# Computing three more MLP units with seven half-size products instead of eight

## The chip, the cores and the metric

The kernel runs on one core of one Trainium2 chip. The metric is the device time of one execution in microseconds (us); several executions are timed and their median is taken. The time before is 2046.41 us, the median of 3 runs (2046.17 to 2046.44).

## The reference

Two blocks follow each other on one sequence of T = 512 tokens of width D = 1024, everything in float32. The first has two layers of sparse attention, a short convolution, a gated merge and an MLP; the second has one layer of dilated attention, an mLSTM and a gated FFN. Cut to what the change touches:

```
# first_block, for each of two layers
x = x + merged @ w_mix_out[l]
u = rmsnorm(x, norm_mlp[l])
x = x + square(relu(u @ w_mlp_up[l])) @ w_mlp_down[l]        # hidden width 4096
# second_block, its FFN
h = modulate(rms_norm(x, g_ffn), sh_f, sc_f)
x = x + gt_f * ((silu(h @ w_gate) * (h @ w_up)) @ w_down)    # hidden width 2816
```

## The kernel before, in words

Activations are kept transposed: x is eight tiles x[0] to x[7] of 128 (of D) by 512 (tokens). A float32 product is made of three float32r matmuls: each operand is split into hi (rounded to float32r) and lo (the rest), and hi·hi, hi·lo and lo·hi are summed in PSUM. The moving operand is a pair (hi, lo) of activations; the weights are loaded as raw blocks of 128x1024 numbers (512 rows by 256 columns), and `split` (L208) makes their hi by a cast on ScalarE (L222, tile wh) and their lo by a subtraction on VectorE (L223, tile wl). Pool whp holds four such pairs, pool rawp eight raw blocks, pool mmp four PSUM banks.

`linear` (L242) is the plain product: for each output tile, k = 0 to 7 and three matmuls of 512 columns each (L290 to L292). `seven` (L311) computes the same for a 2x2 arrangement of half-size blocks (K halved, tokens halved, two blocks of 256 output columns) with seven block products of 24 matmuls of 256 columns each (L412 to L414). Its weight operands are the raw blocks a, b (first 256 columns, upper and lower half of K), c, d (second 256 columns) and sums of them, tile ws; its moving operands are the plain halves of the activation and two mixed ones, ta[k] and tb[k] for k = 0 to 3. `mix` (L480) makes these of x[k] and x[k+4]: four VectorE steps of 128x256 (L487 to L490), then two hi casts on ScalarE (L466) and two lo subtractions on VectorE (L467). ta[3] and tb[3] need x[7], the last tile of the layer before.

The norm of an MLP is applied late: the tiles of u are x times the gain alone (`prep` L469, hi L474 on ScalarE and lo L475 on VectorE), and 1/rms, a column per token, is applied when a hidden tile is read from PSUM. For it `square` (L498) sums the squares of the eight tiles (L505 on ScalarE, L506 on VectorE), `rstd1` (L508) adds them over partitions on TensorE (L1072), takes the root on ScalarE (L513) and refines it on VectorE (L526 to L528), and `rstd2` (L518) spreads it over partitions by a matmul (L1083) and copies it to SBUF (L522).

An MLP has eight units of 512 hidden columns. Units 1 to 7 are computed by `seven` (`up`, L977) and interleaved with the down products of the unit before (`mesh`). Unit 0 is a plain `linear` (u0, L1002): the mixes of k = 0 to 2 are made while the last tiles of w_mix_out come out (`evmix`, L924), the mix of k = 3 in the background of unit 0 (L1005). The FFN has 11 units of 256 gate and 256 up columns; unit 0 and unit 1 are plain (`gateup`, L1551, unit 0 in two halves of tokens since the norm arrives in halves), the others are by `seven`. In the FFN the mixes are made in the background of gateup(1). The norm in the FFN is `ffn_norm` (L1154): column sums L1072, L1157 to L1159 on VectorE, a spread L1083, then L1093, L1103 and L1106 per tile.

The program text gives an order of pieces: `Prog.run` walks the list, fetches weights some units ahead and splits them two units ahead. The order on each engine is then settled by a scheduler when the program is built; each engine works through its queue in that order, and waits on semaphores for the others.

Of the kernel before, what the change touches and what calls it, by code (L numbers as in the profile page):

```python
# [15 lines left out]
P = 128  # L16
# [4 lines left out]
KT = D // P  # L21
# [105 lines left out]
def blocks_kernel(ctx: ExitStack, tc: tile.TileContext, a: dict, out: bass.AP, stop=None):  # L127
# [21 lines left out]
    def slot(dt=F32, w=T):  # L149
        return gp.tile([P, w], dt, tag="g", name=nm("g"))  # L150
# [157 lines left out]

        return ap.unsqueeze(1).to_broadcast([P, 2, H])

    def seven(srcs, xs, ta, tb, evac):  # L311

# [41 lines left out]
            4: {"make": lambda: raw["d"]},  # L356
        }

        def half(d, k0, t):
            return lambda k: [o[:, th(t)] for o in d(k0 + k)]  # L360

        def keep(n, b):
            def f():
                tmp[n] = slot()
                act.copy(tmp[n], bank[b])
            return f
# [18 lines left out]
        def e4():  # L385
            evac(1, 0, bank.pop("Y"), False)

        prods = [
            (1, "X", half(xs, 0, 0), keep(1, "X")),
            (5, "Z", half(ta, 0, 0), keep(5, "Z")),  # L390
            (6, "Y", half(tb, 0, 0), e6),
# [4 lines left out]
        ]  # L396
        pieces = []
        for n, b, mv, after in prods:
            first = n in (1, 5, 6)
            u = us[n]  # L400
            piece = [("unit", u)]
            for m in range(2):

                def emit(u=u, b=b, mv=mv, m=m, first=first):
                    if first and m == 0:
                        bank[b] = mmbank()
                    ps = bank[b][:, th(m)]
                    for k in range(4):
                        hi, lo = mv(k)
                        wh = u["hi"][:, k, m * P : (m + 1) * P]  # L410
                        wl = u["lo"][:, k, m * P : (m + 1) * P]
                        pe.matmul(ps, wh, hi, start=first and m == 0 and k == 0, stop=False, skip_group_check=True)  # L412
                        pe.matmul(ps, wh, lo, start=False, stop=False, skip_group_check=True)  # L413
                        S["pe"] = pe.matmul(ps, wl, hi, start=False, stop=k == 3, skip_group_check=True)  # L414

                piece.append(("do", emit))
            piece.append(("do", after))
            pieces.append(piece)
# [269 lines left out]
    def layer1(l, nextprep):  # L688
# [235 lines left out]
        def evmix(g):  # L924
            def f(j, ps, cs):
                j = 4 * g + j
                dve.tensor_add(x[j], ps, x[j])
                prep("n", j, col(C_NMLP + 8 * l + j))
                if 4 <= j < KT - 1:
                    for step in mix("n", j - 4, y):  # L930
                        step()
            return f
# [12 lines left out]

        NU = MLP_TILES // 4
        W_up = a["w_mlp_up"][l]

        def ev0(j, ps, cs):
            r = slot()  # L950
            dve.scalar_tensor_tensor(r, ps, 0.0, S["n", "rs"], op0=ALU.max, op1=ALU.mult)
            act.activation(r, r, AF.Square)
            hid[j] = hilo(r)

        def evup(c):
            def f(n, t, src, own):
# [18 lines left out]
            return f  # L975

        def up(c):  # L977
            return seven([(W_up, 512 * c), (W_up, 512 * c + 256)], xs, lambda k: S["n", "ta", k], lambda k: S["n", "tb", k], evup(c))

        def down(c, gs=(0, 1), n=1, last=False):  # L980

# [17 lines left out]
                S.pop(("n", "ta", k))  # L999
                S.pop(("n", "tb", k))  # L1000

        u0 = linear(W_up, 0, [4, 4], 0, [P] * 4, xs, ev0)  # L1002
        add(u0[:1])
        do(lambda: rstd1("n"))
        I.append(("bg", mix("n", 3, y)))  # L1005
        add(u0[1:3])
        do(lambda: rstd2("n"))
        add(u0[3:])
        I.append(("drain", None))
        do(ada_start)  # L1010
        I.append(("rate", 0.25))
        I.append(("bg", [ada(n) for n in range(24 * l, 24 * l + 24)] + ([ada_end] if l else [])))
# [150 lines left out]
    def block2():  # L1163
# [440 lines left out]
        def unit(c):  # L1604

            gt = {}

            def evac(n, t, src, own):
                if n == 0:
                    gt[t] = slot()  # L1610
                    act.activation(gt[t], src, AF.Silu)
                    if ("late", t) in gt:
                        finish_(t, *gt.pop(("late", t)))
                elif t in gt:
                    finish_(t, src, own)
                else:
                    gt["late", t] = (src, own)

            def finish_(t, src, own):
                r = gt.pop(t)  # L1620
                dve.tensor_mul(r, src, r)
                for m in range(2):
                    k_ = 2 * c + m
                    if k_ not in ff:
                        ff[k_] = (slot(F32R), slot(F32R))
                    hi, lo = ff[k_]
                    act.copy(hi[:, th(t)], r[:, th(m)])
                    dve.tensor_sub(lo[:, th(t)], r[:, th(m)], hi[:, th(t)].bitcast(F32))

            return seven([(a["w_gate_2"], 256 * c), (a["w_up_2"], 256 * c)], xs, lambda k: S["h", "ta", k],  # L1630
                         lambda k: S["h", "tb", k], evac)

        NG = FF_TILES // 2
        ND = (FF_TILES + 3) // 4
# [25 lines left out]
        add(u0[:2])  # L1660
        do(lambda: S.pop("rest")())
        I.append(("ahead", (3, 6)))
        add(u0[2:])
        I.append(("rate", 2.0))
        I.append(("bg", [f for k in range(4) for f in mix("h", k, lambda j: S.pop(("h", "y", j)))]))
        add(gateup(1, 1))
        I.append(("drain", None))
        I.append(("ahead", (2, 5)))
        for c in range(2, NG - 1, 2):
            I.extend(mesh(unit(c) + unit(c + 1), down(c // 2 - 1)))  # L1670
        I.extend(mesh(unit(NG - 1), down(ND - 2)))
# [107 lines left out]
```

## Time and profile before

| | |
|---|---|
| median of 3 runs | 2046.41 us |
| the profiled execution | 2044.83 us |
| its span, first to last instruction | 2043.0 us |
| TensorE busy | 2026.1 us, 99% |
| VectorE busy | 1547.0 us, 76% |
| ScalarE busy | 986.6 us, 48% |
| mean granted TensorE clock | 0.997 |

Matmuls are pipelined: a row's duration is longer than the distance to the next row, so the pace of TensorE is read from one start to the next. The same holds, by about 0.09 us, for VectorE and ScalarE. The clock column is the share of 2.4 GHz that was granted; 0.50 is 1.2 GHz.

### The profile page before, as it was taken

To read this page: it belongs to the slowest core of one execution; us is meant where nothing else is said; L and a number is where in the kernel's file an instruction comes from. 1 tells how busy PE (TensorE), PEld (TensorE's weight loads), DVE (VectorE), ACT (ScalarE), POOL (GpSimd) and SP (SyncE) were. 2 spreads that over 40 slices of the span, in tenths; PEclk is the share of its full clock that TensorE was granted. 3 is DMA by queue.
4 is the path that set the end of the run, shared out by engine and by line. 5 is a ranking of instruction groups with operands and counts; after the bars stand their busy time and mean duration, and the time that the engine had idled before them with its cause. 6 is when DMAs were issued, how large, how long until landed. Compare 5 with 4: busy or idle time off the path is not lost.

```text
span 2043.0 us, 29780 instructions
## 1 busy us (share of the span) xinstructions
PE 2026.1 (99%) x11632; PEld 1754.7 (86%) x11632; DVE 1547.0 (76%) x2783; ACT 986.6 (48%) x1713; POOL 19.5 (1%) x33
## 2 busy tenths in 40 slices
PE   9999999999999999999999999999999998999999
PEld 7888888899999888888888999999877797999998
DVE  6998667888787659977678888877777386777775
ACT  5323774644444432338655444455377754444442
POOL 0000000000000000000000000000010000000000
PEclk9999999999999999999999999999999999999999
DMA  7233223344444332331224444443221131332321
GB/s 248 83 94 102 73 63 93 100 149 149 150 155 147 105 105 83 100 96 63 73 93 134 145 155 134 155 134 88 87 83 54 50 114 32 104 103 94 114 94 42
DMA packets 203116, 216.62 MB, mean 106 GB/s; under 512 B 10720, under 2 KB 182112, under 8 KB 202976
## 3 DMA queue, kind: packets, MB, share of 16 engines
q1 hardware_dynamic: 202976, 214.73, 33.8%
q8 instruction: 91, 1.49, 0.3%
q14 instruction: 49, 0.40, 0.1%
HBM read 212.60 MB, written 2.10 MB: 105 GB/s over the span
## 4 chain that ended last, share of the span: by engine, by line
PE 95%; DVE 2%; ACT 1%; DMA 0%; issue 0%; SPq 0%; POOL 0%; DVEq 0%; ACTq 0%; POOLq 0%
PE mm L290 14%; PE mm L291 13%; PE mm L292 13%; PE mm L414 7%; PE mm L413 7%; PE mm L412 7%; PE at L290 7%; PE at L291 7%; PE at L292 7%; PE at L555 2%; PE mm L441 1%; PE mm L442 1%; PE mm L443 1%; PE ot L589 1%; PE at L574 1%; PE mm L1583 1%
## 5 line engine op out<-in xcount | busy, mean ns | idle before, releaser
L222 ACT CAST wh<-raw 128x1024 fp32r<-128x1024 f32 (+3 forms) x278 | 283.6, 1023 | 535.0 <-PE mm L413 221.6
L290 PE MATMUL mm<-g,wh 128*128 128x512 f32 (+2 forms) x1360 | 512.6, 378 | 1.7 <-ACT g L1103 1.6
L292 PE MATMUL mm<-g,wl 128*128 128x512 f32 (+2 forms) x1360 | 512.9, 377 | 0.0
L291 PE MATMUL mm<-g,wh 128*128 128x512 f32 (+2 forms) x1360 | 510.4, 375 | 0.0
L223 DVE TENSOR_TENSOR wl<-raw,wh 128x1024 fp32r<-128x1024 f32 (+3 forms) x278 | 329.3, 1186 | 141.3 <-ACT wh L222 140.3
L414 PE MATMUL mm<-g,wl 128*128 128x256 f32 x1288 | 364.6, 283 | 0.0
L413 PE MATMUL mm<-g,wh 128*128 128x256 f32 x1288 | 364.5, 283 | 0.0
L412 PE MATMUL mm<-g,wh 128*128 128x256 f32 x1288 | 363.9, 283 | 0.0
L290 PEld LDWEIGHTS mm<-g,wh 128*128 128x128 f32 x1360 | 255.8, 188 | 49.6 <-issue 4.3
L292 PEld LDWEIGHTS mm<-g,wl 128*128 128x128 f32 x1360 | 256.2, 188 | 45.5 <-issue 1.0
L291 PEld LDWEIGHTS mm<-g,wh 128*128 128x128 f32 x1360 | 256.1, 188 | 44.2 <-DVE g L475 0.3
L412 PEld LDWEIGHTS mm<-g,wh 128*128 128x128 f32 x1288 | 246.8, 192 | 4.7
L413 PEld LDWEIGHTS mm<-g,wh 128*128 128x128 f32 x1288 | 246.8, 192 | 4.6
L414 PEld LDWEIGHTS mm<-g,wl 128*128 128x128 f32 x1288 | 246.8, 192 | 0.2
L290 PE MATMUL at<-g,g 128*128 128x512 f32 x592 | 231.9, 392 | 0.0
L291 PE MATMUL at<-g,g 128*128 128x512 f32 x592 | 231.8, 392 | 0.0
L292 PE MATMUL at<-g,g 128*128 128x512 f32 x592 | 230.6, 389 | 0.1
L222 ACT CAST wh<-ws 128x1024 fp32r<-128x1024 f32 x69 | 72.3, 1048 | 182.3 <-PE mm L413 170.1
L292 PEld LDWEIGHTS at<-g,g 128*128 128x128 f32 x592 | 111.2, 188 | 24.7 <-DVE g L223 0.8
L223 DVE TENSOR_TENSOR wl<-ws,wh 128x1024 fp32r<-128x1024 f32 x69 | 84.5, 1224 | 59.7 <-ACT wh L222 59.7
L290 PEld LDWEIGHTS at<-g,g 128*128 128x128 f32 x592 | 111.7, 189 | 19.9
L291 PEld LDWEIGHTS at<-g,g 128*128 128x128 f32 x592 | 111.7, 189 | 18.6
(272 smaller groups left out, 2685.4 us busy)
## 6 DMA issues: line engine op xcount, KB each, us to landing
raw<-w_in SPq DMA_DIRECT2D x111, 512.0 KB, 3.8
raw<-w_mlp_up SPq DMA_DIRECT2D x64, 512.0 KB, 3.8
raw<-w_mlp_down SPq DMA_DIRECT2D x64, 512.0 KB, 3.6
g<-w_ada SPq DMA_DIRECT2D x96, 256.0 KB, 4.2
raw<-w_gate SPq DMA_DIRECT2D x22, 512.0 KB, 3.7
raw<-w_up SPq DMA_DIRECT2D x22, 512.0 KB, 3.6
raw<-w_down SPq DMA_DIRECT2D x22, 512.0 KB, 3.4
raw<-w_mix_out SPq DMA_DIRECT2D x16, 512.0 KB, 3.7
```

Of the source, the lines that this page charges most:

```text
L222: act.copy(hi, raw)
L223: dve.tensor_sub(lo, raw, hi.bitcast(F32))
L290: pe.matmul(ps, wh, hi[:, cs], start=st, stop=False)
L291: pe.matmul(ps, wh, lo[:, cs], start=False, stop=False)
L292: S["pe"] = pe.matmul(ps, wl, hi[:, cs], start=False, stop=en)
L412: pe.matmul(ps, wh, hi, start=first and m == 0 and k == 0, stop=False, skip_group_check=True)
L413: pe.matmul(ps, wh, lo, start=False, stop=False, skip_group_check=True)
L414: S["pe"] = pe.matmul(ps, wl, hi, start=False, stop=k == 3, skip_group_check=True)
L441: pe.matmul(ps, xh, wh, start=kb + k == 0, stop=False)
L442: pe.matmul(ps, xl, wh, start=False, stop=False)
L443: pe.matmul(ps, xh, wl, start=False, stop=kb + k == KT - 1)
L555: pe.matmul(ps[:, :WM], qs[hh][:, i * P : (i + 1) * P], ks[hh][n][:, :WM], start=n == 0, stop=n == 1)
```

## The change

`seven` gets a flag `late`, with another order of products and other weight sums: products 1, 2 and 3 come first (they need plain activations only), 5, 6, 7 and 4 after them, and product 3 takes a bank of its own. b - the lower half of the first columns - is turned in place into the operand of product 3. Unit 0 of both MLPs becomes `up(0)` with this flag, and the second FFN unit `unit(1)`. The mix of k = 3 moves from the background of unit 0 to the reading of x[7], and the FFN's mixes from the background of gateup(1) to places beside the second half of gateup(0).

```
+        def p2late():
+            dve.tensor_add(raw["b"], raw["b"], raw["a"])
+            dve.tensor_add(raw["b"], raw["b"], ws["s"])
+        if late:
+            us = {
+                1: {"load": get("a", "c"), "make": lambda: raw["a"]},
+                2: {"load": get("d", "b"), "make": lambda: raw["b"], "post": lambda: (p1(), p2late())},
+                3: {"make": lambda: raw["b"]},
+                5: {"make": lambda: ws["s"], "post": p5},
+                6: {"make": lambda: ws["s"], "post": p6},
+                7: {"make": lambda: raw["c"]},
+                4: {"make": lambda: raw["d"]},
+            }
...
+            (1, "X", half(xs, 0, 0), keep(1, "X")),
+            (2, "X", half(xs, 4, 0), e2),
+            (3, "Z", half(xs, 4, 1), lambda: None),
+            (5, "V", half(ta, 0, 0), e5late),
+            (6, "Y", half(tb, 0, 0), e6late),
+            (7, "Y", half(ta, 0, 1), e7),
+            (4, "Y", half(tb, 0, 1), e4),
+        ] if late else [
...
-                if 4 <= j < KT - 1:
+                if j >= 4:
                     for step in mix("n", j - 4, y):
...
-        u0 = linear(W_up, 0, [4, 4], 0, [P] * 4, xs, ev0)
-        add(u0[:1])
+        u0 = up(0)
+        I.extend(u0[0])
         do(lambda: rstd1("n"))
-        I.append(("bg", mix("n", 3, y)))
-        add(u0[1:3])
+        I.extend(u0[1][:-1])
         do(lambda: rstd2("n"))
-        add(u0[3:])
-        I.append(("drain", None))
+        I.extend(u0[1][-1:])
+        add(u0[2:])
...
-        add(u0[2:])
-        I.append(("rate", 2.0))
-        I.append(("bg", [f for k in range(4) for f in mix("h", k, lambda j: S.pop(("h", "y", j)))]))
-        add(gateup(1, 1))
-        I.append(("drain", None))
+        add(u0[2:10])
         I.append(("ahead", (2, 5)))
+        for c in range(4):
+            for f in mix("h", c, lambda j: S.pop(("h", "y", j))):
+                do(f)
+            add(u0[10 + 2 * c : 12 + 2 * c if c < 3 else None])
+        add(unit(1))
```

`e6late` combines the results of products 1, 5, 6 and 3 in three VectorE steps, a copy and a subtraction. In the changed kernel line numbers behind L311 are some 30 higher: L412 to L414 are L448 to L450, L467 is L503, L475 is L511, L506 is L542, L512 is L548, L927 is L963, L487 to L490 are L523 to L526, L1072 is L1102, L1083 is L1113, L1157 is L1187. L361 and L362 are the two sums of `p2late`, L342 is `p5`.

The order that the scheduler settles, at three places. First VectorE in layer 1, around the residual add of x[7] (x_102; x_101 is x[6]). Before:

```order
L475 SCALAR_TENSOR_TENSOR g_3336<-x_101,cols,g_3335 128x512
L506 TENSOR_TENSOR g_3121<-g_3121,g_3339 128x512
L487 TENSOR_TENSOR g_3346<-g_3342 128x256
L927 TENSOR_TENSOR x_102<-mm_3368,x_102 128x512
L488 TENSOR_TENSOR g_3347<-g_3344,g_3346 128x256
L489 TENSOR_TENSOR g_3346<-g_3342,g_3344 128x256
L490 TENSOR_TENSOR g_3347<-g_3344,g_3347 128x256
L223 TENSOR_TENSOR wl_3450<-raw_3303,wh_3449 128x1024
L467 TENSOR_TENSOR g_3353<-g_3346,g_3352 128x512
L467 TENSOR_TENSOR g_3357<-g_3347,g_3356 128x512
L475 SCALAR_TENSOR_TENSOR g_3395<-x_102,cols,g_3394 128x512
```

With the change (g_3353 and g_3357 are again the lo of ta[2] and tb[2]; the rows ahead of these are L361 between the adds of x[5] and x[6], then L362 and the split of the operand of product 3):

```order
L963 TENSOR_TENSOR x_102<-mm_3368,x_102 128x512
L542 TENSOR_TENSOR g_3121<-g_3121,g_3339 128x512
L523 TENSOR_TENSOR g_3346<-g_3342 128x256
L223 TENSOR_TENSOR wl_3465<-ws_3364,wh_3464 128x1024
L524 TENSOR_TENSOR g_3347<-g_3344,g_3346 128x256
L525 TENSOR_TENSOR g_3346<-g_3342,g_3344 128x256
L526 TENSOR_TENSOR g_3347<-g_3344,g_3347 128x256
L342 TENSOR_TENSOR ws_3364<-ws_3364,raw_3143 128x1024
L503 TENSOR_TENSOR g_3353<-g_3346,g_3352 128x512
L503 TENSOR_TENSOR g_3357<-g_3347,g_3356 128x512
L223 TENSOR_TENSOR wl_3518<-ws_3364,wh_3517 128x1024
L511 SCALAR_TENSOR_TENSOR g_3395<-x_102,cols,g_3394 128x512
```

Between the add of x[7] and its lo stood one operation of 128x1024; now three do.

Second, TensorE at the same place. Before, the unit's 25th matmul is followed by the column sums, and everything to there needs x[0] to x[3] only:

```order
L291 MATMUL mm_3434<-g_3183,wh_3305 128x512
L292 MATMUL mm_3434<-g_3182,wl_3306 128x512
L290 MATMUL mm_3471<-g_3117,wh_3364 128x512
L1072 MATMUL at_3420<-rdc,g_3121 128x1 x4
L291 MATMUL mm_3471<-g_3118,wh_3364 128x512
```

With the change, after 24 matmuls of product 1, nine of product 3 (bank mm_3522) and six of product 5 (bank mm_3553), come these (mm_3586 is product 6; g_3352 and g_3353 are hi and lo of ta[2], g_3394 is the hi of x[7]):

```order
L448 MATMUL mm_3553<-g_3352,wh_3464 128x256
L449 MATMUL mm_3553<-g_3353,wh_3464 128x256
L450 MATMUL mm_3553<-g_3352,wl_3465 128x256
L448 MATMUL mm_3586<-g_3246,wh_3517 128x256
L449 MATMUL mm_3586<-g_3247,wh_3517 128x256
L448 MATMUL mm_3522<-g_3394,wh_3419 128x256
L450 MATMUL mm_3586<-g_3246,wl_3518 128x256
L448 MATMUL mm_3586<-g_3301,wh_3517 128x256
```

The scheduler has put the 24 matmuls of product 2 behind the column sums and product 5: the mixed operands are reached after 39 matmuls of the unit. Behind the rows shown come ten more up to the column sums (L1102), then nine of product 3, one of product 6 and fifteen of product 5, the first of these with ta[3], one of product 6, the 24 of product 2, the spread (L1113), fourteen of product 6, and then unit 1's first product with a new bank.

Third, VectorE in the FFN's norm, from the last residual add of the second half to the reciprocal. Before:

```order
L1528 SCALAR_TENSOR_TENSOR x_102<-mm_16244,modc,x_102 128x256
L1106 SCALAR_TENSOR_TENSOR g_16200<-g_16188,modc,g_16199 128x256
L223 TENSOR_TENSOR wl_16526<-raw_16390,wh_16525 128x1024
L506 TENSOR_TENSOR g_15934<-g_15934,g_16270 128x256
L223 TENSOR_TENSOR wl_16657<-raw_16409,wh_16656 128x1024
L506 TENSOR_TENSOR g_15934<-g_15934,g_16286 128x256
L506 TENSOR_TENSOR g_15934<-g_15934,g_16302 128x256
L506 TENSOR_TENSOR g_15934<-g_15934,g_16318 128x256
L1157 TENSOR_SCALAR n_3338_16325<-at_16321 128x2
L1159 RECIPROCAL n_3337_16324<-n_3337_16324 128x2
```

With the change:

```order
L361 TENSOR_TENSOR raw_16332<-raw_16332,raw_16290 128x1024
L1136 SCALAR_TENSOR_TENSOR g_16414<-g_16402,modc,g_16413 128x256
L362 TENSOR_TENSOR raw_16332<-raw_16332,ws_16625 128x1024
L542 TENSOR_TENSOR g_16144<-g_16144,g_16484 128x256
L542 TENSOR_TENSOR g_16144<-g_16144,g_16500 128x256
L542 TENSOR_TENSOR g_16144<-g_16144,g_16516 128x256
L223 TENSOR_TENSOR wl_16734<-raw_16332,wh_16733 128x1024
L542 TENSOR_TENSOR g_16144<-g_16144,g_16532 128x256
L223 TENSOR_TENSOR wl_16948<-ws_16625,wh_16947 128x1024
L1187 TENSOR_SCALAR n_3354_16539<-at_16535 128x2
L342 TENSOR_TENSOR ws_16625<-ws_16625,raw_16290 128x1024
L1189 RECIPROCAL n_3353_16538<-n_3353_16538 128x2
```

Behind the last add two operations of 128x1024 stood ahead of the reciprocal; now there are five, one of them between L1187 and the reciprocal.

## Rows read from the trace of the kernel before

**Rows 1.** The page: busy time, share of the span and instructions of each engine.
```profile
PE 2026.1 (99%) x11632; PEld 1754.7 (86%) x11632; DVE 1547.0 (76%) x2783; ACT 986.6 (48%) x1713; POOL 19.5 (1%) x33
```

**Rows 2.** TensorE's waits, whole span: total us, times, longest us.
```profile
PE mm L1583 <- ACT g L1591: 5.4, 1, 5.4
...
PE mm L290 <- ACT g L1103: 1.6, 1, 1.6
...
PE at L1083 <- DVE g L1081: 1.2, 1, 1.2
```

**Rows 3.** By stage (unit 0): us; PE, PEld, DVE, ACT, POOL busy (count); clock, DMA share, GB/s.
```profile
364.76:388.42 23.66, 23.66 (x108) 19.22 (x106) 18.57 (x34) 13.94 (x21) 0.00 (x0) 1.00 0.15 45
1069.44:1093.10 23.66, 23.66 (x127) 20.24 (x128) 17.88 (x30) 13.19 (x19) 0.00 (x0) 1.00 0.17 51
```

**Rows 4.** Timeline of TensorE: start us, us, then the instruction.
```profile
345.04 0.39 PE L290 MATMUL mm<-g,wh 128*128 128x512 f32 x1
...
370.20 0.39 PE L290 MATMUL mm<-g,wh 128*128 128x512 f32 x1
...
388.42 0.28 PE L412 MATMUL mm<-g,wh 128*128 128x256 f32 x1
...
394.29 0.28 PE L413 MATMUL mm<-g,wh 128*128 128x256 f32 x1
```

**Rows 5.** Timeline of VectorE, from x[5]'s residual add to x[7]'s.
```profile
354.08 0.69 DVE L927 TENSOR_TENSOR x<-mm,x 128x512 f32<-128x512 f32 x1 [0.24 <-PE mm L292]
...
359.83 0.69 DVE L927 TENSOR_TENSOR x<-mm,x 128x512 f32<-128x512 f32 x1
360.43 1.22 DVE L223 TENSOR_TENSOR wl<-raw,wh 128x1024 fp32r<-128x1024 f32 x1
361.57 1.29 DVE L467 TENSOR_TENSOR g<-g,g 128x512 fp32r<-128x512 f32 x2
362.77 0.74 DVE L475 SCALAR_TENSOR_TENSOR g<-x,cols,g 128x512 fp32r<-128x512 f32 x1
...
364.96 0.69 DVE L927 TENSOR_TENSOR x<-mm,x 128x512 f32<-128x512 f32 x1 [0.51 <-PE mm L292]
365.57 0.42 DVE L488 TENSOR_TENSOR g<-g,g 128x256 f32<-128x256 f32 x1
365.90 0.42 DVE L489 TENSOR_TENSOR g<-g,g 128x256 f32<-128x256 f32 x1
```

**Rows 6.** ScalarE's groups from 359.8 to 385 us: busy us, mean ns.
```profile
L466 ACT CAST g<-g 128x512 fp32r<-128x512 f32 x8 | 4.6, 616 | 0.6 <-DVE g L489 0.5
L222 ACT CAST wh<-raw 128x1024 fp32r<-128x1024 f32 x3 | 3.2, 1051 | 2.6 <-issue 1.3 <-ACT g L936 1.0 <-PE mm L291 0.3
```

**Rows 7.** The chain that ended last (start us, us): layer 1's column sums and spread.
```profile
370.60 0.84 PE at L1072 x8
377.25 0.86 PE at L1083 x2
```

**Rows 8.** Timelines in the FFN's norm, VectorE and then TensorE.
```profile
1685.78 1.48 DVE L506 TENSOR_TENSOR g<-g,g 128x256 f32<-128x256 f32 x3
1687.95 0.16 DVE L1157 TENSOR_SCALAR n<-at 128x2 f32<-128x2 f32 x1 [0.70 <-PE at L1072]
1688.44 0.17 DVE L1159 RECIPROCAL n<-n 128x2 f32<-128x2 f32 x1 [0.33 <-ACT n L1158]
...
1689.86 0.67 PE L1083 MATMUL at<-g,kon 128*128 128x256 f32 x2 [1.25 <-DVE g L1081]
```

**Rows 9.** By stage around two waits of TensorE: columns as in rows 3.
```profile
1415.74:1419.14 3.40, 3.40 (x18) 3.31 (x17) 1.18 (x4) 0.15 (x1) 0.00 (x0) 0.50 0.00 0
1419.20:1422.60 3.40, 3.40 (x30) 3.37 (x29) 3.07 (x8) 2.55 (x8) 0.00 (x0) 1.00 0.00 0
...
1691.30:1695.00 3.70, 3.70 (x32) 3.67 (x31) 3.18 (x8) 3.16 (x9) 0.00 (x0) 1.00 0.02 4
```

**Rows 10.** The chain that ended last, layer 2's first down products.
```profile
1096.57 1.38 DVE g L1044 x4
```

More of the change, by code (lines that the diff above doesn't have):

```diff
@@ L309, in both, with seven @@
         return ap.unsqueeze(1).to_broadcast([P, 2, H])
-    def seven(srcs, xs, ta, tb, evac):
+    def seven(srcs, xs, ta, tb, evac, late=False):
         raw = {}
@@ L386, in e4, with e5late, e6late @@
             evac(1, 0, bank.pop("Y"), False)
-        prods = [
+        def e5late():
+            keep(5, "V")()
+            bank.pop("V")
+        def e6late():
+            u = tmp.pop(1)
+            dve.tensor_sub(u, bank["Y"], u)
+            act.copy(bank["Y"], u)
+            dve.tensor_sub(u, tmp[5], u)
+            dve.tensor_add(u, bank.pop("Z"), u)
+            evac(0, 1, u, True)
+        prods = [
+            (1, "X", half(xs, 0, 0), keep(1, "X")),
[6 more added lines that the diff above has]
+        ] if late else [
             (1, "X", half(xs, 0, 0), keep(1, "X")),
@@ L398, in seven @@
         for n, b, mv, after in prods:
-            first = n in (1, 5, 6)
+            first = n in (1, 5, 6) or late and n == 3
             u = us[n]
@@ L947, in layer1 @@
         W_up = a["w_mlp_up"][l]
[L949 to L953, printed above, removed]
         def evup(c):
@@ L977, in up @@
         def up(c):
-            return seven([(W_up, 512 * c), (W_up, 512 * c + 256)], xs, lambda k: S["n", "ta", k], lambda k: S["n", "tb", k], evup(c))
+            return seven([(W_up, 512 * c), (W_up, 512 * c + 256)], xs, lambda k: S["n", "ta", k], lambda k: S["n", "tb", k],
+                         evup(c), late=c == 0)
         def down(c, gs=(0, 1), n=1, last=False):
@@ L1630, in unit @@
             return seven([(a["w_gate_2"], 256 * c), (a["w_up_2"], 256 * c)], xs, lambda k: S["h", "ta", k],
-                         lambda k: S["h", "tb", k], evac)
+                         lambda k: S["h", "tb", k], evac, late=c == 1)
         NG = FF_TILES // 2
```

## Prediction

> **What bounds the kernel now.** I read the busy times first. TensorE is busy 2026.1 us of the 2043.0 us span, VectorE 1547.0 [rows 1]: the time is TensorE's queue, and VectorE is the engine with the least slack behind it. Next TensorE's waits, the view that says how full that queue is: in the whole program only three are over 1 us and end on ScalarE or VectorE once the work runs, 5.4, 1.6 and 1.2 us [rows 2]. The 1.2 us one lies in the FFN's norm, which the change moves work into; no wait lies in the unit that the change replaces. So each column of matmul taken out of the two places in the MLPs and the one in the FFN is worth its full time, as long as TensorE stays fed. That is the second thing to read, by stage: in both MLP places TensorE is busy 23.66 of 23.66 us, and VectorE already 18.57 and 17.88 us of them [rows 3]. VectorE has some 5 us to spare in each, and the change gives it work in just this stretch.
>
> **TensorE's saving.** The unit before is 4 tiles x 8 k x 3 = 96 matmuls of 512 columns; by seven products it is 7 x 2 x 4 x 3 = 168 of 256. Paces are read start to start: from 345.04 to 370.20 us stand 111 intervals of the wide kind, 0.2267 us each, and from 388.42 to 394.29 us 49 of the narrow, 0.1198 us each [rows 4]. So 96 x 0.2267 = 21.76 us become 168 x 0.1198 = 20.13, 1.63 less. gateup(1) has the same 96, so three units give 4.9 us.
>
> The Trainium skill (TensorE: Matmul & The Clock Gate, section "Wait — 56ns, not 53.3ns?") gives a warm start-to-start of N/2.4 plus about 2.5 ns, an estimate of 215.7 and 109.2 ns here. By that rule a unit would save 20.71 - 18.35 = 2.36 us and the three 7.1. The trace does not agree (226.7 and 119.8 ns, some 10 ns more on each matmul, which narrow ones pay twice as often) [rows 4], and the measurement decides.
>
> **What VectorE gets.** A unit by seven products splits seven weight blocks in place of four and forms five block sums: three splits and five sums more, eight operations of 128x1024. Such an operation occupies VectorE 1.14 us start to start (360.43 to 361.57), one of 128x512 0.60, the gained x less its hi, L475, 0.66 (0.74 less the 0.08 by which 1.22 overlaps), one of 128x256 0.33 [rows 5]. So 8 x 1.14 = 9.1 us of new work meet some 5 us of room, and part of them stands in the queue ahead of the very operands that TensorE needs next. On ScalarE a split's cast takes 1.05 us, three more per unit; it has 13.94 of 23.66 us busy [rows 3, 6].
>
> **Layer 1's start, laid out by the new order and these paces** (change's lines; times are those of the trace before). Between x[5]'s residual add at 354.08 and x[6]'s at 359.83 lie 5.75 us [rows 5], and the new queue there, the sum L361 with it, takes 0.60 + 1.20 + 2 x 1.14 + 0.66 + 0.60 + 0.33 = 5.7, so x[6]'s add starts as before. Behind it five 1024-wide operations stand before x[7]'s lo, where two stood:
> - add 0.60, three mix steps 1.0, sum L362 1.14, two lo's 1.20, split 1.14, lo of x[6] 0.66: x[7]'s add starts at 365.57 (364.96 before).
> - add 0.60, square sum 0.60 after a wait for ScalarE's square, which stands behind two casts there (bounds 0 and 0.62, one cast of 512 [rows 6]; I take the middle, 0.3), mix step 0.33, split 1.14, three mix steps 1.0, sum L342 1.14: the lo of ta[2] starts at 370.68 and lands 0.69 later, at **371.4**.
> - two lo's 1.20, split 1.14 lands at **373.1**; lo of x[7] ends at 373.8.
>
> TensorE starts the unit at 364.76. The new order gives it product 1 (24), then k 0 to 2 of product 3 (9) and k 0 and 1 of product 5 (6): 39 x 0.12 = 4.7 us, to 369.45. The name of the change lets one expect 72 matmuls of plain operands, 8.6 us, but the queue reaches ta[2] after 39. **First wait:** 369.45 to 371.4, less one matmul that needs only hi: 1.8 us. **Second:** five matmuls fit between 371.4 and 373.1, where the split of product 6's weights lands: 1.1 us. **Third:** 11 matmuls and the column sums (0.84 us [rows 7]) bring TensorE to 375.3; the sums' reader L548 stands ahead of the mix steps of ta[3] in VectorE's queue, so 0.2 + 1.0 + four rstd steps 0.8 + lo 0.69 give 378.0; ten more matmuls last to 376.5: 1.4 us. **Fourth:** the late order holds four banks (X, Z, V, Y) of a pool of four, so unit 1's first product waits until X is read. After 378.0: 39 matmuls, the spread (0.86 us [rows 7]), 14 matmuls, to 385.3. X's last product ends at 382.9; its reader stands behind ScalarE's cast of the next weights (1.05 [rows 6]) and VectorE's split of them (1.14) and takes 0.69: about 386.0 with the hand-overs, so 0.7 us. Sum 5.0 us, against 1.63 saved: **+3.4 us**. What hid such chains before is the cover: 21.8 us of matmuls with one square sum to wait for. Layer 2 has the same order, tile for tile, and VectorE's load is within 4% [rows 3]: **+3.4 us** again. Bounds of a layer's waits: 4.0 us without the 0.3 and the fourth wait; 6.5 with 0.62 in place of 0.3 and if the sum before x[6] finds no room (1.14). I take 5.0, the steps as laid out.
>
> **FFN.** VectorE's queue of the second half's norm now holds L361, L362 and two splits behind the last residual add, and L342 between L1187 and L1189; before there were two splits and nothing between. Two splits before, at 1683.17 and 1684.64; the reciprocal's 0.33 us of waiting and the 0.70 us before L1157 hide part of the new ones [rows 8]. Up to the column sums that is one operation of 1.14 us more, less 0.4 of pauses among the square sums (three in 1.48 us at 1685.78, 1.08 at full pace): +0.7; behind them a split in a wait of 0.70, +0.4; then 1.14 in a wait of 0.33, +0.8: 1.9 us later (0.8 if the split that no longer stands between the adds lets them come a place earlier). TensorE's wait for the spread, 1.25 us [rows 8], becomes about 3.1. The mixes for unit 1 move from the background to places beside part 2 of gateup(0), where TensorE is ahead and VectorE waits on it; I cost them at nothing, at 16 x 0.33 + 8 x 0.60 = 10 us of VectorE if that cover were gone. Less 1.63: **+0.3 us**. DMA loads keep number and size, only some change places on SP; with DMA busy 0.15 and 0.17 in the stretches [rows 3] I cost that at nothing.
>
> **TensorE's clock.** After the 1.62 us wait at 1414.37 [rows 2, 9] the granted clock stood at 0.50 (1.2 GHz) from 1415.74 for 3.4 us, and 18 matmuls started in it where the 3.4 us after had 30 at 2.4 GHz [rows 9]: 12/30 of 3.4, 1.4 us lost. The first two new waits together idle TensorE for 2.9 us of four, more than that. I take one such stretch per MLP at its full price, since the column sums behind it lie on the chain to ta[3]: **+2.8 us**.
>
> **Sum.** +3.4 + 3.4 + 0.3 + 2.8 = +9.9 us. The profiled execution took 2044.83 us for its span of 2043.0, so 2054.7; the median of the runs, 2046.41, lies 1.6 above it, so I forecast **2056.3 us**.
>
> **Rivals.**
> - *The clock holds* (2053.5): the same waits without the slow stretch, +7.1. For it: after the 1.25 us wait at 1689.86, TensorE still had 1.00 [rows 8, 9]. Against it: four waits follow each other within 17 us, and the worst two are closer than that. The Trainium skill (TensorE: Matmul & The Clock Gate, section "Why this matters for your kernels") warns of long idle gaps between bursts; by it, waits of under 2 us each would leave the clock up, which is this case, and the row of the 1.62 us wait does not agree.
> - *More of the same* (2060.5): a second slow stretch in each MLP (+2.8) and, in layer 2, unit 1's operands behind VectorE's w_ada sums, which stand on the chain that ended last there, 1.38 us for four steps [rows 10]: 9.9 + 2.8 + 1.4 = +14.1. Against it: the later units of an MLP by seven products run without a wait over 1 us today [rows 2].
> - *Break-even* (2047): only the first wait is real, because VectorE's queue runs ahead behind it: 2 x (1.8 - 1.63) + 0.3.
> - *The matmuls alone count* (faster, 2041.5): VectorE's room before x[6] takes the sums, ta[2] is there by 369.45 and the rest follows. It decides at 1.9 us: two of the four 1024-wide operations between x[6]'s add and ta[2] would have to be done earlier. Against it: between x[6]'s add and x[7]'s VectorE has only 0.51 us idle [rows 5], and gets more.
>
> **How the numbers follow.** Forecast 0.45, clock holds 0.25, more of the same 0.17, break-even 0.09, matmuls alone 0.04. About 0.2% (4 us) is what a measurement of this kernel tells from no change; the first three lie above it: slower 0.87, same 0.09, faster 0.04. The range leaves out break-even, the faster case and a little at the top: its low end is the clock holding with the waits at 4.0 us per layer and 0.8 us in the FFN, 2 x 2.37 - 0.83 = +3.9, so 2050.3; its high end is the third case with the waits at their upper bound, 2 x 1.5 more, 2063.5.
>
> **What would show it.** Right: in the profile after, TensorE waits on VectorE's lo of ta (L503) and on split L223 near 370 and 1069 us, with three to five waits of 0.5 to 2 us; it waits about 3 us for the spread L1113 in the FFN; its narrow matmuls replace 288 wide ones; the clock's share falls a little. Wrong: no wait on L503 there, the clock at 1.00 through both starts, or unit 1 beginning without a wait on a bank.

## The result, and the profile after

The changed kernel takes 2060.69 us (median of 4 runs, 2060.26 to 2061.49), the kernel before beside it 2046.29: 14.4 us more, ratio 1.0075 with a 95% interval of 1.0063 to 1.0087. That is slower, inside the stated range (2050.3 to 2063.5), and 4.4 us above the forecast of 2056.3. The profiled execution took 2061.03 us for a span of 2059.0, 16.0 more than the span before.

The page, busy times (beside [rows 1]), and TensorE's waits over the whole span, us in total, times, longest (beside [rows 2]):

```profile
PE 2031.6 (99%) x11848; PEld 1768.2 (86%) x11848; DVE 1581.3 (77%) x2829; ACT 1000.1 (49%) x1741; POOL 19.5 (1%) x33
```

```profile
PE mm L1613 <- ACT g L1621: 3.7, 1, 3.7
PE at L1113 <- DVE g L1111: 3.1, 1, 3.1
PE mm L449 <- DVE g L503: 2.6, 3, 1.0
PE at L292 <- DVE g L223: 2.6, 2, 1.3
...
PE at L1102 <- DVE g L542: 1.4, 3, 0.8
PE mm L448 <- ACT g L502: 1.4, 3, 0.7
PE mm L448 <- DVE g L988: 0.9, 2, 0.4
```

VectorE has 34 us more to do. The 4.9 us that the narrower matmuls save are not seen in TensorE's busy time, since it counts matmuls at half clock for their longer time, and the part of a loss at a wait that the brackets below leave out. The list holds the waits that were forecast (L503 and L988 in the MLPs, L1113 in the FFN) and others that were not: L502, the hi cast of a mixed operand on ScalarE; L1102 on a square sum; and L292 on L223, a down product waiting for the lo of its weights.

Where the 16 us came in is read by laying the two timelines against each other at instructions that are the same in both:

| start of | before | after | later by |
|---|---|---|---|
| unit 0 of layer 1 | 364.76 | 364.53 | -0.23 |
| unit 0 of layer 2 | 1062.88 | 1069.72 | +6.84 |
| the matmul behind the 1.62 us wait [rows 2] | 1414.37 | 1430.37 | +16.00 |
| a matmul of w_out, shortly ahead of the FFN's norm | 1672.75 | 1687.32 | +14.57 |
| FFN unit 2, some way in | 1739.85 | 1755.79 | +15.94 |

So layer 1's MLP costs 7.1 us, layer 2's 9.2, the FFN 1.4, and 1.4 came back in between, where the trace before had a slow stretch of the clock [rows 9] and the one after has none.

Layer 1's unit 0, TensorE: start us, us, instruction, wait and what ended it.

```profile
369.08 0.28 PE L450 MATMUL mm<-g,wl 128*128 128x256 f32 x1
369.72 0.38 PE L448 MATMUL mm<-g,wh 128*128 128x256 f32 x1 [0.36 <-ACT g L502]
371.14 0.39 PE L449 MATMUL mm<-g,wh 128*128 128x256 f32 x1 [1.04 <-DVE g L503]
...
372.95 0.39 PE L450 MATMUL mm<-g,wl 128*128 128x256 f32 x1 [0.25 <-DVE wl L223]
...
376.23 0.40 PE L450 MATMUL mm<-g,wl 128*128 128x256 f32 x2
377.32 0.38 PE L448 MATMUL mm<-g,wh 128*128 128x256 f32 x1 [0.69 <-ACT g L502]
378.23 0.58 PE L449 MATMUL mm<-g,wh 128*128 128x256 f32 x1 [0.53 <-DVE g L503]
...
386.77 0.28 PE L450 MATMUL mm<-g,wl 128*128 128x256 f32 x1
387.49 0.36 PE L448 MATMUL mm<-g,wh 128*128 128x256 f32 x1 [0.45 <-DVE g L988]
```

The loss at a wait is the distance between starts less 0.12 us for each matmul that ran in it; it is more than the bracket, which leaves hand-overs out. First wait: 371.14 - 369.08 - 2 x 0.12 = 1.82. Second: 372.95 - 371.14 - 5 x 0.12 = 1.21. Third: 378.23 - 376.23 - 3 x 0.12 = 1.64. Fourth: 0.72 - 0.12 = 0.60. The first and the third wait end in two steps, on the hi cast L502 and then on the lo L503. In layer 2 the first, second and fourth are as large; the third falls into the slow stretch of the clock. VectorE at the same place:

```profile
369.27 1.22 DVE L342 TENSOR_TENSOR ws<-ws,raw 128x1024 f32<-128x1024 f32 x1
370.41 1.28 DVE L503 TENSOR_TENSOR g<-g,g 128x512 fp32r<-128x512 f32 x2
371.67 1.22 DVE L223 TENSOR_TENSOR wl<-ws,wh 128x1024 fp32r<-128x1024 f32 x1
372.82 0.74 DVE L511 SCALAR_TENSOR_TENSOR g<-x,cols,g 128x512 fp32r<-128x512 f32 x1
```

VectorE never stops here: the sum L342 stands ahead of the lo of ta[2], which was forecast to start at 370.68 and starts at 370.41; x[7]'s lo follows at 372.82.

By stage (columns as in [rows 3]): the slow stretch of layer 1 and 3 us behind it, then layer 2's.

```profile
377.90:381.30 3.40, 3.07 (x14) 3.07 (x15) 2.89 (x7) 1.32 (x3) 0.00 (x0) 0.51 0.17 44
381.40:384.40 3.00, 3.00 (x27) 3.00 (x27) 1.23 (x1) 1.05 (x1) 0.00 (x0) 1.00 0.35 119
...
1077.60:1087.90 10.30, 10.12 (x45) 9.56 (x46) 6.90 (x19) 5.76 (x9) 0.00 (x0) 0.50 0.11 39
```

In layer 1 the clock falls to 1.2 GHz in the third wait and stays there for 3.4 us: the 14 matmuls from 378.23 to 381.38 took 3.15 us where 14 take 1.68 at 2.4 GHz, 1.5 us lost. In layer 2, with the same order and the same first two waits, it falls at the second wait already and stays there for 10.3 us. The first product of unit 1 comes 22.96 us after the start of unit 0 in layer 1, and 24.41 in layer 2: 1.45 us for the longer slow stretch.

The wait not forecast, in layer 1: VectorE, then SyncE's loads (start us, time to issue), then TensorE.

```profile
422.39 0.69 DVE L1074 SCALAR_TENSOR_TENSOR g<-g,g 128x512 f32<-128x512 f32 x1 [0.61 <-DMA g<-w_ada]
...
424.45 0.69 DVE L1074 SCALAR_TENSOR_TENSOR g<-g,g 128x512 f32<-128x512 f32 x1 [1.36 <-DMA g<-w_ada]
...
426.34 0.68 DVE L223 TENSOR_TENSOR g<-raw,g 128x512 fp32r<-128x512 f32 x1
```

```profile
408.45 0.38 SPq L187 DMA_DIRECT2D raw<-w_mlp_up  x1
417.14 0.37 SPq L187 DMA_DIRECT2D raw<-w_mlp_down  x1
417.61 0.92 SPq L1073 DMA_DIRECT2D g<-w_ada  x2
```

```profile
427.08 0.50 PE L292 MATMUL at<-g,g 128*128 128x512 f32 x1 [1.29 <-DVE g L223]
```

SyncE issued nothing from 408.8 to 417.1, since its next load, a block of w_mlp_down, had no free buffer yet; two w_ada loads stood behind it. VectorE reached the steps that use them (L1074, background sums that nothing waits for soon) 4.2 us after the issue, before they had landed, idled 0.61 and 1.36 us, and so made a lo of w_mlp_down late. TensorE lost 1.45 us there, and 1.43 at 1127.10 in layer 2. These are the second pair of w_ada loads of the layer. Before, the second pair (L1043) was issued 6.0 us ahead of its first step (L1044), which did not wait:

```profile
406.62 0.92 SPq L1043 DMA_DIRECT2D g<-w_ada  x2
...
412.67 0.68 DVE L1044 SCALAR_TENSOR_TENSOR g<-g,g 128x512 f32<-128x512 f32 x1
```

### The profile page after: what moved, and what is told of

Its sections match the earlier page's. It is cut to its first block, busy times and chain, and to the rows that moved or that the text cites. A ratio compares the mean times of both kernels' runs of the same rounds, so it can differ in the third digit from the quotient of the medians.

```text
span 2059.0 us, 30303 instructions
## 1 busy us (share of the span) xinstructions
PE 2031.6 (99%) x11848; PEld 1768.2 (86%) x11848; DVE 1581.3 (77%) x2829; ACT 1000.1 (49%) x1741; POOL 19.5 (1%) x33
## 4 chain that ended last, share of the span: by engine, by line
PE 91%; DVE 4%; ACT 2%; DMA 1%; issue 1%; SPq 0%; POOL 0%; DVEq 0%; ACTq 0%; POOLq 0%
PE mm L290 13%; PE mm L291 13%; PE mm L292 13%; PE mm L449 8%; PE mm L450 8%; PE mm L448 8%; PE at L290 6%; PE at L291 6%; PE at L292 6%; PE at L591 1%; PE mm L477 1%; PE mm L478 1%; PE mm L479 1%; PE ot L625 1%; PE at L610 1%; DVE wl L223 1%
## 5 line engine op out<-in xcount | busy, mean ns | idle before, releaser
L222 ACT CAST wh<-raw 128x1024 fp32r<-128x1024 f32 (+2 forms) x281 | 286.9, 1024 | 538.1 <-PE mm L449 225.4
L290 PE MATMUL mm<-g,wh 128*128 128x512 f32 (+3 forms) x1296 | 486.9, 377 | 2.1 <-ACT g L1133 1.6
L292 PE MATMUL mm<-g,wl 128*128 128x512 f32 (+3 forms) x1296 | 486.0, 375 | 0.0
L291 PE MATMUL mm<-g,wh 128*128 128x512 f32 (+3 forms) x1296 | 484.4, 374 | 0.0
L223 DVE TENSOR_TENSOR wl<-raw,wh 128x1024 fp32r<-128x1024 f32 (+2 forms) x281 | 332.6, 1185 | 147.1 <-ACT wh L222 145.7
L449 PE MATMUL mm<-g,wh 128*128 128x256 f32 x1456 | 414.9, 285 | 2.6 <-DVE g L503 2.6
L448 PE MATMUL mm<-g,wh 128*128 128x256 f32 x1456 | 413.9, 285 | 3.2 <-ACT g L502 1.4
L450 PE MATMUL mm<-g,wl 128*128 128x256 f32 x1456 | 413.6, 285 | 0.4 <-DVE wl L223 0.4
L448 PEld LDWEIGHTS mm<-g,wh 128*128 128x128 f32 x1456 | 280.8, 193 | 10.1 <-ACT g L502 2.0
L449 PEld LDWEIGHTS mm<-g,wh 128*128 128x128 f32 x1456 | 281.0, 193 | 8.7 <-DVE g L503 3.5
L290 PEld LDWEIGHTS mm<-g,wh 128*128 128x128 f32 (+1 forms) x1296 | 243.2, 188 | 47.1 <-issue 3.8
L450 PEld LDWEIGHTS mm<-g,wl 128*128 128x128 f32 x1456 | 281.0, 193 | 1.8 <-DVE wl L223 0.9
L292 PEld LDWEIGHTS mm<-g,wl 128*128 128x128 f32 (+1 forms) x1296 | 243.4, 188 | 42.7 <-issue 0.5
L291 PEld LDWEIGHTS mm<-g,wh 128*128 128x128 f32 (+1 forms) x1296 | 243.4, 188 | 41.1 <-issue 0.2
L292 PE MATMUL at<-g,g 128*128 128x512 f32 x592 | 231.0, 390 | 2.7 <-DVE g L223 2.6
L292 PEld LDWEIGHTS at<-g,g 128*128 128x128 f32 x592 | 111.2, 188 | 27.6 <-DVE g L223 3.7
L223 DVE TENSOR_TENSOR wl<-ws,wh 128x1024 fp32r<-128x1024 f32 x75 | 91.7, 1223 | 49.6 <-ACT wh L222 49.6
```

Of the source, the lines that this page charges most:

```text
L222: act.copy(hi, raw)
L223: dve.tensor_sub(lo, raw, hi.bitcast(F32))
L290: pe.matmul(ps, wh, hi[:, cs], start=st, stop=False)
L291: pe.matmul(ps, wh, lo[:, cs], start=False, stop=False)
L292: S["pe"] = pe.matmul(ps, wl, hi[:, cs], start=False, stop=en)
```

## The experiments

Medians in us against the kernel before on the same chip; e1 to e4 share its runs, so do e5 to e8, and e9 to e12.

| run | median | before | more by | ratio, 95% interval |
|---|---|---|---|---|
| e1 MLPs only | 2061.87 | 2045.18 | +16.7 | 1.0081, 1.0064 to 1.0098 |
| e2 FFN only | 2046.31 | 2045.18 | +1.1 | 1.0005, 0.9996 to 1.0015 |
| e3 copy early | 2053.55 | 2045.18 | +8.4 | 1.0046, 1.0031 to 1.0061 |
| e4 w_ada by GpSimd | 2057.58 | 2045.18 | +12.4 | 1.0064, 1.0049 to 1.0079 |
| e5 sums on GpSimd | 2078.66 | 2044.58 | +34.1 | 1.0163, 1.0148 to 1.0178 |
| e6 two sums left out | 2054.30 | 2044.58 | +9.7 | 1.0048, 1.0033 to 1.0063 |
| e7 e3 and e4 | 2050.60 | 2044.58 | +6.0 | 1.0029, 1.0016 to 1.0041 |
| e8 e3, e4 and e5 | 2064.97 | 2044.58 | +20.4 | 1.0097, 1.0081 to 1.0112 |
| e9 before, other banks | 2038.87 | 2045.23 | -6.4 | 0.9968, 0.9957 to 0.9980 |
| e10 e9, splits later | 2036.09 | 2045.23 | -9.1 | 0.9954, 0.9941 to 0.9968 |
| e11 MLPs only, k outside | 2048.00 | 2045.23 | +2.8 | 1.0012, 1.0003 to 1.0021 |
| e12 change, other banks | 2058.12 | 2045.23 | +12.9 | 1.0064, 1.0049 to 1.0078 |

**e1 and e2: one place at a time.** e1 has `late` and the seven products in the MLPs only, e2 in the FFN only; the rest is as before.

> Unit 0 of both MLPs by seven products, the FFN as before. The traces of before and after, laid against each other, put +7.1 us into layer 1's MLP, +9.2 into layer 2's and +1.4 into the FFN; a slow stretch of the clock at 1416 us in the trace of before, 1.5 us, is missing after. Theory A (each place pays for itself, by its own waits): before plus 14 to 16 us, 2060 to 2062. Rival B (the places are coupled: the FFN pays more because the MLPs end later, or gains what they lose): more than 2 us away from after less 1.4.

> Only the FFN's unit 1 by seven products, both MLPs as before. Theory A: before plus 1.4 us, 2047.7, with the wait for the spread at about 3.1 us as in the trace after. Rival B (the prediction's sum for the FFN, a longer wait that the shorter matmuls pay for): +0.3, 2046.6. Rival C (FFN alone is faster, the loss of after at this place comes from the clock that the MLPs upset): 2044.7 or less.

The MLPs alone cost +16.7, the FFN alone +1.1. e1's median fits two of its cases: it lies in theory A's 2060 to 2062, and also 2.6 us from after less 1.4, which is rival B's. Its trace speaks for A: the first wait in layer 1 costs 1.82 us again, and the wait for the spread in the FFN is 1.2 us as before. What e1 has more is clock: the long slow stretch comes in both layers, and the mean clock is 0.991 for 0.994. Layer 1:

```profile
372.60:382.50 9.90, 9.51 (x41) 8.92 (x42) 6.59 (x17) 5.84 (x9) 0.00 (x0) 0.50 0.11 37
```

e2 is theory A by its trace, which has the wait forecast for the spread; its interval is too wide to tell +1.4 from +0.3.

```profile
PE mm L1620 <- ACT g L1628: 3.3, 1, 3.3
PE at L1120 <- DVE g L1118: 3.1, 1, 3.1
```

**e3: what TensorE has in hand.** Product 2 adds to the bank that holds product 1, and so waits for `keep`, the copy of product 1 on ScalarE (L381). After the change that copy ran at 378.64, behind the casts of the mixed operands.

```
-                    for step in mix("n", j - 4, y):
-                        step()
+                    first, second = mix("n", j - 4, y)
+                    first()
+                    if j < 6:
+                        second()
+                    else:
+                        pend.append(second)
...
+            with tc.issue_after(S["keep"].ins):
+                for f in pend:
+                    f()
```

> The copy of product 1 out of its bank is put ahead of the casts of ta[2], tb[2], ta[3] and tb[3] in ScalarE's queue, so that product 2 (24 matmuls, nine of which need neither x[7] nor a mix) can start behind product 1; nothing else. Theory A (TensorE starves because product 2 waits for this copy, which ScalarE reaches only 11 us after product 1 ended): the first wait shrinks from 1.8 us to under 0.9 and some of the later ones too, in both layers: 3 to 5 us less than after, 2056 to 2058. Rival B (VectorE's amount of work sets the time, whatever TensorE has in hand): the waits move behind, total within 1 us of after.

It is 8.4 above before, 6 less than the change, more than expected. The order explains it, and not quite as the expectation had it: with the casts behind the copy, the lo's of ta[2] and ta[3] went back too. VectorE in layer 1 of e3:

```profile
368.81 0.75 DVE L511 SCALAR_TENSOR_TENSOR g<-x,cols,g 128x512 fp32r<-128x512 f32 x1
...
371.44 1.22 DVE L342 TENSOR_TENSOR ws<-ws,raw 128x1024 f32<-128x1024 f32 x1
...
374.26 0.69 DVE L503 TENSOR_TENSOR g<-g,g 128x512 fp32r<-128x512 f32 x1
```

x[7]'s lo now comes 4 us earlier (368.81 for 372.82), ahead of L342 and ta[2]; the column sums come at 370.30 for 374.37, and behind them stand the rest of product 3 and all of product 2, 33 matmuls that need nothing mixed, while VectorE makes the mixed operands. Layer 1's waits in this unit fall to

```profile
PE mm L449 <- DVE g L503: 0.8, 1, 0.8
PE mm L449 <- DVE g L511: 0.6, 1, 0.6
PE mm L448 <- DVE g L994: 0.6, 1, 0.6
```

and the clock holds at 1.00 from 364 to 395 us in e3, and from 1060 to 1100. The matmul behind the 1.62 us wait starts at 1421.61, 7.2 us later than before, where the change had it 16.0 later. Of these 8.8 us, 4.4 are the two slow stretches (1.5 and 2.9) that did not come; the rest is shorter waits. So the amount of VectorE work alone does not fix the time; what TensorE can do meanwhile counts.

**e4: the w_ada loads.** In `ada`, `nc.sync.dma_start` becomes `nc.gpsimd.dma_start`.

> The loads of w_ada are issued by GpSimd in place of SP, in both layers; nothing else. After has a wait of 1.3 us on the lo of a w_mlp_down block in each MLP, near 427 and 1127 us, behind VectorE steps that idle for w_ada loads. Theory A (these loads are late because they stand on SP behind raw loads that wait for a free raw buffer): both waits go, 2.5 to 3 us less than after, 2057.7 to 2058.2. Rival B (VectorE is late by its backlog and the loads only fill the gap): within 0.7 us of after. Rival C (loads that come earlier put the w_ada sums ahead of steps that TensorE needs sooner): slower than after.

In its trace TensorE has no listed wait from 395 to 440 and from 1100 to 1140 us: both are gone, which is theory A's mechanism. The median is 2.0 us nearer to before than the change was. The trace shows why that single number is a poor measure: this time layer 1 has the long slow stretch and layer 2 the short one.

```profile
373.50:383.60 10.10, 9.76 (x47) 9.47 (x47) 5.82 (x17) 5.32 (x8) 0.55 (x1) 0.51 0.27 89
1082.80:1086.20 3.40, 3.09 (x14) 3.09 (x15) 2.87 (x7) 1.30 (x3) 0.63 (x1) 0.55 0.42 127
```

The four executions of e4 took 2054.0, 2056.0, 2059.2 and 2060.6 us, in the order of their mean clock: 0.996, 0.995, 0.993, 0.992.

**e5 and e6: the sums on VectorE.** e5 moves the five block sums of a late unit to GpSimd (`dve.tensor_add` becomes `nc.gpsimd.tensor_add`); e6 drops the two of `p2late`.

> The five block sums of the three late units (L339, L342, L345, L361, L362 of the change) run on GpSimd in place of VectorE; nothing else. GpSimd is idle there; no trace here shows what it takes for 128x1024, so that is read first. Theory A (the sums in VectorE's queue, three of them ahead of x[7]'s lo, make the mixed operands late): if GpSimd takes up to 3 us per sum, the waits on ta[2] and ta[3] in the MLPs and the 3.1 us wait for the spread in the FFN shrink by 1 us or more each; 4 to 9 us less than after, 2052 to 2057. Rival B (it is the product that needs a copied bank, and the weights' own splits, that TensorE lacks): within 2 us of after. Rival C (a sum on GpSimd takes so long, or slows VectorE beside it so much, that the operands of products 3, 5 and 6 come later still): slower than after.

> The sums L361 and L362 of the late units are left out (2.3 us of VectorE in each of three units; the operand of product 3 is then another block, so product 3 isn't computed as in the reference); nothing else. Theory A: x[7]'s add and everything behind it on VectorE starts up to 2.3 us earlier, less what VectorE then waits for TensorE: 1 to 2 us less wait per MLP, 1.5 in the FFN: 3 to 6 us less than after. Rival B (the queue ahead of ta[2] is limited by x[6] and x[7], not by the sums): within 1.5 us of after.

e6 is theory A by its number: 4.7 less than the change, x[7]'s lo at 369.89 for 372.82, the wait for the spread 1.9 for 3.1. Part of it is the clock, which holds at 1.00 in layer 1 of e6. e5 is rival C, by far. One of GpSimd's groups, its sums L361 and L362 in layer 1, then VectorE beside them:

```profile
L339 POOL TENSOR_TENSOR ws<-raw,raw 128x1024 f32<-128x1024 f32 x3 | 8.1, 2689 | 214.2 <-DMA raw<-w_mlp_up 115.5 <-DMA raw<-w_up 98.7
...
356.05 2.77 POOL L361 TENSOR_TENSOR raw<-raw,raw 128x1024 f32<-128x1024 f32 x1 [28.79 <-DVE wl L223]
358.90 2.73 POOL L362 TENSOR_TENSOR raw<-raw,ws 128x1024 f32<-128x1024 f32 x1
```

```profile
356.49 2.88 DVE L511 SCALAR_TENSOR_TENSOR g<-x,cols,g 128x512 fp32r<-128x512 f32 x1
359.30 2.88 DVE L542 TENSOR_TENSOR g<-g,g 128x512 f32<-128x512 f32 x1
```

A sum takes GpSimd some 2.7 us where VectorE took 1.22 (L342 above), and VectorE's steps beside it took 2.88 in place of the 0.75 and 0.69 that the same lines take 10 us later, when GpSimd is idle: both engines lose.

**e7 and e8: causes together.**

> The early copy of product 1 and the w_ada loads on GpSimd together. The early copy alone gave before plus 8.4 us, and its trace still has waits of 1.1 us on a lo of w_mlp_down; the loads on GpSimd alone took both such waits away. Theory A (two separate causes, which add up): 2 to 3 us less than the early copy alone, before plus 5.4 to 6.4. Rival B (the loads were late only because the units before ended late): no more than 0.7 us less than the early copy alone.

> Early copy, w_ada loads on GpSimd and the five sums on GpSimd. If the waits have the three causes named and no other, little is left but the 1.63 us that each unit saves: between 2 us faster and 2 us slower than before. Rival (VectorE's splits and the x[7] chain alone are too slow for a unit that starts with 72 plain matmuls, whatever else is moved): before plus 3 us or more.

e7 is +6.0 where e3 was +8.4: theory A, the two causes add. The intervals of the two overlap; what decides is that e3 still waits 2.8 us in all for a lo of w_mlp_down (L292 on L223), and that e7's list has no such wait. e8 (+20.4) carries e5's loss, with which its expectation did not reckon: neither of its two cases was the reason.

**e9 and e10: the FFN without the change.** The longest wait of the kernel before, 5.4 us [rows 2], stands in this stretch, and the change only shortened it to 3.7. e9 gives the second half of gateup(0) idle banks; e10 adds that gateup(1)'s splits queue behind the norm.

```
-                                    bank[wch, j] = mmbank()
+                                    other = nparts == 2 and cs.start
+                                    bank[wch, j] = atbank() if other and wch == "g" else otbank() if other and not j else mmbank()
```

> The kernel before, with none of the change; in gateup(0) the second half of the tokens takes three of its four banks from the other two pools (two from atp, one from otp), which are idle there. In the trace before, TensorE waits 5.4 us for the first of these banks, which a Silu frees that stands on ScalarE behind 24 steps of the norm. Theory A (the wait is for the bank alone): it goes, 4 to 6 us faster than before. Rival B (the operands of the second half are late as well, or VectorE's work moves into the gap): less than 1.5 us faster.

> As the run before, and the two weight splits of gateup(1) that stand in VectorE's queue among the square sums of the norm's second half are put behind the norm's last step ahead of the spread. Theory A (work of 1024 elements in that queue delays the spread, as L361, L362 and L342 do in the change): the wait of 1.25 us for the spread falls to under 0.5, 1 to 2 us less than the run before, 5 to 8 us faster than before. Rival B (the splits are then late for gateup(1)): no gain over the run before.

Theory A twice, with gains somewhat above those expected: 6.4 us, and 2.8 more in e10. In e9 the first matmul in a new bank (tile at) follows without a wait:

```profile
1699.37 0.28 PE L1586 MATMUL mm<-g,g 128*128 128x256 f32 x1
1699.49 0.28 PE L1584 MATMUL at<-g,g 128*128 128x256 f32 x1
```

The clock reads 1.00 from 1690 to 1710 us, where before read 0.53 around this wait:

```profile
1698.70:1705.50 6.80, 3.27 (x15) 3.27 (x16) 4.29 (x11) 4.46 (x10) 0.00 (x0) 0.53 0.00 0
```

That is part of the 6.4. In e10 the wait for the spread is down from 1.25 [rows 8] to 0.17, which is 1.1 of its 2.8; the rest is open:

```profile
1686.78 0.67 PE L1088 MATMUL at<-g,kon 128*128 128x256 f32 x2 [0.17 <-DVE g L1086]
```

e10, 2036.09 us, beats both kernels, by 9.1 and by some 24 us, and contains nothing of the change.

**e11: as many plain matmuls as there are.** In late units, with e3's and e4's edits and the FFN as before:

```
-            for m in range(2):
...
-                    for k in range(4):
+                    for k in range(4):
...
+                        for m in range(2):
```

> Only the MLPs by seven products, the FFN as before; early copy, w_ada loads by GpSimd, and in the late units the loop over k outside that over the two halves of a block, so that k = 0 to 2 of both halves can run ahead of x[7]: 24 + 18 + 18 matmuls that need neither x[7] nor a mix, in place of 24 + 9. Theory A (TensorE lacks only operands that are there but stand behind late ones): the two MLPs together cost nothing or gain up to 3 us. Rival B (VectorE's 9.1 us of new work per unit meet 5 us of room, so TensorE waits whatever its order): before plus 2.5 to 5 us, the waits now on splits (L223) and at the end of the unit.

+2.8, where the MLPs of the change cost +16.7 by themselves. Two waits are left in each layer, and no slow stretch in either. Layer 1, and the stretch with the unit:

```profile
PE mm L449 <- ACT mm L411: 1.2, 1, 1.2
PE mm L450 <- DVE g L519: 0.8, 1, 0.8
```

```profile
364.00:388.00 24.00, 22.01 (x168) 20.37 (x167) 22.69 (x41) 18.23 (x28) 1.22 (x2) 1.00 0.37 112
```

VectorE is busy 22.69 of 24.00 us. The number is rival B's, but neither wait ends on a split: one ends on a lo of a mixed operand (L519), the other on a copy back into a bank on ScalarE (L411, in `e6late` between two VectorE steps). The three edits together - copy, loads and order - took away some 14 of the 16.7 us, slow stretches included; e7 against e3 puts 2.4 of them to the loads. In what is left, each unit still loses more at its waits than the 1.63 us it saves. That VectorE and ScalarE have too much to do for less is argued from their busy times, not shown.

**e12: the banks under the change.** The diff of e9 on the changed kernel.

> The change, with the three banks of the run on before. Theory A (what the banks give is independent of the unit that follows): 4 to 6 us less than after. Rival B (with unit 1 by seven products VectorE sets the pace behind the norm, the 4 us that TensorE gains turn into waits in unit 1): 1 to 3 us less than after, with new waits on steps of VectorE in unit 1.

Rival B: 12.9 above before for 14.4, a gain of 1.5 where e9 gave 6.4; the size is loose, since e12's executions spread from 2055.1 to 2062.9. The wait on the bank is gone and a new one stands in unit 1, for the lo of a mixed operand:

```profile
1735.98 0.39 PE L449 MATMUL mm<-g,wh 128*128 128x256 f32 x1 [1.37 <-DVE g L503]
```

In the kernel before, the plain unit 1 was the cover under which the mixes were made; the change has spent it.

## Why the prediction was right, and where it was off

- **What bounds the kernel, and the direction.** Right. TensorE's queue was full, VectorE had the least slack, and unit 0 was cover. One slip of reading: the second row of [rows 3] begins 6.6 us too late, since unit 0 of layer 2 runs from 1062.88 to 1086.53. VectorE is busy 18.57 of 23.65 us there, as in layer 1, so the conclusion stands. Of the signs that it named, four waits of 0.6 to 1.8 us, 3.06 us for the spread and a lower clock share (0.994 for 0.997) came; none of the signs of being wrong did.
- **The four waits of a layer.** Forecast 1.8, 1.1, 1.4 and 0.7, sum 5.0; measured in layer 1 1.82, 1.21, 1.64 and 0.60, sum 5.27. The layout by queue order and start-to-start paces held to 0.3 us, though two of the waits also ended on ScalarE's hi cast, which the layout took as done. That the order counts, and not the amount of work alone, is shown by e3; e11 points the same way, with the loads moved as well. e6 shows that work ahead of x[7]'s lo counts too.
- **The clock.** One slow stretch per MLP was right for layer 1 (1.5 us, forecast 1.4) and too small for layer 2, where it lasted 10.3 us and cost some 1.4 more. "The clock holds" fell in this trace; in e3, e7 and e11, with shorter waits, it did hold.
- **DMA loads "cost at nothing".** The step that failed. "Only some change places on SP" was the point: w_ada loads moved behind loads that wait for buffers, VectorE waits for them in order, and TensorE lost 1.45 and 1.43 us. e4 took both waits away, e7 shows that they add to the rest. The rival "more of the same" named the w_ada sums, and its 2060.5 lies nearest to the measured 2060.69, but in part for another reason: it put them on the path of unit 1's operands; it was the loads of these sums, in both layers. Its second slow stretch per MLP came in layer 2 alone, as one stretch of three times the length.
- **Short waits.** Some 0.5 us in layer 1 and 1.2 in layer 2 behind the unit (0.7 of it on a copy L381) were not in the sum.
- **FFN, +0.3.** The wait for the spread came as forecast (3.06 for 3.1). Missed were 0.83 us on the square sums of the norm's first half, 0.35 on those of the second, and 3.4 us more at half clock; against them the wait for the bank fell from 5.4 to 3.7. Together +1.4, in e2 +1.1 with an interval that takes in zero.
- **What came back.** The slow stretch at 1416 us, which the forecast left in place as part of before, was absent after: -1.4 in the traces. The change does not decide it: e1, e3, e4 and e7, which hold its MLPs too, have one there again.

So the forecast of +9.9 was short by the w_ada loads (2.9), the slow stretches (1.5), the short waits (1.7), the FFN (1.1) and 0.3 for each layer's unit, and over by the 1.4 that came back. In the traces that makes 9.9 + 2.9 + 1.5 + 1.7 + 1.1 + 0.6 - 1.4 = 16.3, against 16.2 measured. The medians give +14.4, because the profiled execution before lay 1.5 us below this median and the one after 0.3 above its own.

The number inside the range is in part luck. The terms that were too small add up to 7.8 us; on the forecast of 2056.3 that makes some 2064, above the range. The 1.4 that came back, and the way the profiled executions lay to their medians (1.6 below it before, which the forecast had added on top, and 0.3 above it after), brought it down to 2060.69. The direction and the four waits are no luck: they came where they were laid out.

What stays open: why the clock fell for 3.4 us in one layer and 10.3 in the other. e4 had it the other way round, and e1 had the long stretch in both, so it is not the layer. In these traces the long stretch began at the second wait or within half a us behind it, and the short one at the third; what decides between them no run shows.

## What to carry to other kernels

Count the cover, not only the work: a stage that keeps TensorE busy on operands that are already there may be worth more than the matmuls it wastes, because the next stage's operands are made under it. When a block of work moves, read every in-order queue it touches to the end, the DMA issuer's too: a load behind one that waits for a buffer delays whoever reaches its consumer first. And look at the longest wait of the stretch before shortening its work; here three PSUM banks from idle pools and a later place for some weight splits gave 9.1 us.

## What the runs showed of the hardware that was not expected

- GpSimd beside VectorE: while GpSimd added two blocks of 128x1024, two-input steps of VectorE of 0.75 and 0.69 us took 2.88 each (e5). The Trainium skill (GPSIMD Engine Reference, section "1. Specifications") says that GpSimd shares its SBUF interfaces with VectorE and contends with VectorE instructions that have two inputs in SBUF; the rows agree, and put a factor of about four on it.
- The granted clock after the same wait: behind the 1.62 us wait of the norm, before had 3.4 us at 0.50 [rows 9]. After, the same wait ends at 1430.37, and the stretch reads 1.00:

```profile
1430.00:1436.00 6.00, 5.63 (x44) 5.48 (x45) 4.92 (x15) 3.10 (x9) 0.00 (x0) 1.00 0.02 4
```

One wait of a given length therefore does not tell whether the clock falls; in e4 the mean clock alone ordered four executions over 6.5 us.
